# The recurrent block's weights split ahead of time and kept in DRAM, GpSimd taken out of that block, and the first gate's modulation summed on TensorE

## The chip, the core and the metric

One program on one core of a Trainium2 chip. The metric is the device time of one execution in microseconds (us). All matrix work is float32 in value: TensorE is fed pairs of `float32r` tiles (a high part and the remainder), three products for each pair of operands.

## The reference, cut to what matters

Two layers on a latent stream and a context stream of 256 tokens each, D = 1024. Layer 0 mixes by retention, layer 1 by a bidirectional gated linear recurrence (RG-LRU); each is followed by a gated ConvFFN. Every mixer and FFN is modulated by rows computed from `c`.

```python
for i in range(DEPTH):                       # DEPTH = 2; kind 0 = retention, kind 1 = RG-LRU
    mod_l = (silu(c) @ ada_w[i] + ada_b[i]); mod_c = silu(c_ctx) @ ada_w[i] + ada_b[i]
    sh1, sc1, g1, sh2, sc2, g2 = split(mod_l, 6)          # the same for the context
    h = rmsnorm(x, norm_mix[i]) * (1 + sc1) + sh1
    x = x + g1 * mixer(h)
    x = x + g2 * conv_ffn(rmsnorm(x, norm_ffn[i]) * (1 + sc2) + sh2)
return rmsnorm(x, final_norm)

def lru_mixer(h):                            # LRU_WIDTH = 1280, 8 blocks of 160
    y_br, x_br = split(h @ w_in, 2); x_br = dwconv4(x_br)
    for d in (forward, backward):
        r, i = sigmoid(block_diag(gate_w[d]) @ x_br + gate_b[d])
        log_a = -8 * r * softplus(-lam[d]); a = exp(log_a)
        h_d = scan(h_t = a_t * h_(t-1) + sqrt(-expm1(2 log_a)) * (i * x_br))
    return ((h_fwd + h_bwd) * gelu(y_br)) @ w_out
def conv_ffn(h): g, v = split(dwconv3(h @ w_up), 2); return (silu(g) * v) @ w_down
```

## The kernel before

All weights lie in DRAM as 128x128 blocks in the order in which TensorE uses them (`BLOCKS`, 1888 of them). Eight blocks make a **unit** (128x1024), two units a **piece** (1 MiB). SP loads pieces into four buffers `raw` (`load_pieces`). For each unit `unit_hi` copies `raw` to `whi`, rounding it, and `unit_lo` writes the remainder `wlo = raw - whi`; there are five buffers of each (`WBUFS`). `mm3` then issues the three matmuls (L431, L432, L433 in the trace). Outside of the recurrent block `prep_units` makes `whi` on ScalarE (ACT) and `wlo` on VectorE (DVE), two or three units ahead of TensorE (`ahead`).

The pieces of the modulation matrix `ada_w` (`ada`, 48 pieces) stand between the weight pieces. For all but the first eight of them (`k`), ACT multiplies each quarter of the piece by one column of silu(c) (`adap`, L486) and GpSimd (POOL) adds the products up (L487); a few matmuls against a one-hot column (L496) then sum over partitions. The groups are `g1`, `f0` in the retention, `l1`, `f1` in the first FFN (`ffn0`). Their work is handed out by `tick`, which every matmul group of eight blocks calls.

The recurrent block (`lru`) runs from 860 to 1038 us of the span. Its order on TensorE is written out by hand (`LRU_SEQ`: `x`, `y` projections, `g` gates, `s` a batch of square roots and gelus), then come 80 blocks of the output projection. Everything else there (convolution taps, gates, scans, and the splitting of the 40 units of weights) is placed by a small list scheduler (`Schedule`), which builds the order of each engine from costs in `add({"act": .., "dve": .., "pool": ..})` and due times; tasks that name several engines go to the one that it finds free. Each instruction stream is then executed in that order.

Of the kernel before, what the change touches and what calls it, by code (L numbers as in the profile page):

```python
# [12 lines left out]
P = 128  # L13
# [82 lines left out]
def make_plan():  # L96
# [57 lines left out]
    ffn(0)  # L154
    mat("lru_in", range(KD), [WCH + c for c in LRU_FIRST[:2]], True)
# [30 lines left out]
class Task:  # L186
    def __init__(self, alts, fn, deps=(), due=0.0, new=(), reads=()):
        self.alts, self.fn, self.deps, self.due = alts, fn, [d for d in deps if d], due
        self.new, self.reads, self.end = list(new), list(reads), None
        for b in self.reads:  # L190
            b.n += 1


class Schedule:
# [19 lines left out]
    def issue(self, t, e, at):  # L214
        self.free[e] = t.end = at + t.alts[e]
# [36 lines left out]
BLOCKS, PIECES = make_plan()  # L252
# [10 lines left out]
class Net:  # L263
    def __init__(self, ctx, tc, wpk, xt, cv, par, cst, out):
# [15 lines left out]
        self.ada_done, self.ada_sum = set(), {}  # L280

# [38 lines left out]
    def tick(self, n=1):  # L320
# [17 lines left out]
    def load_pieces(self, upto):  # L338
        while self.npiece <= min(upto, len(PIECES) - 1):
# [9 lines left out]
            n = PIECE if PIECES[i][0] == "ada" else min(PIECE, (len(BLOCKS) - PIECES[i][1]) * P)  # L349
# [42 lines left out]
    def unit_lo(self, e):  # L392
        r, hi = self.units[self.nlo]
# [6 lines left out]
        self.nlo += 1  # L400

# [12 lines left out]
    def blk(self, key, n=1):  # L414
# [9 lines left out]
        if key[0][:4] == "main":  # L424
            assert self.npiece <= self.piece_of[u // 2] + 4
# [31 lines left out]
    def pass_ada(self, pi):  # L457
        while self.npast < pi:
            p = PIECES[self.npast]
            if p[0] == "ada" and p[1] != "k":  # L460
                self.ada_piece(self.npast)
            self.npast += 1

    def ada_piece(self, pi):
# [12 lines left out]
        if half == 0:  # L477
# [11 lines left out]
        self.adaq.extend((pi, lambda s=s, j=j: product(s, j)) for j in range(4) for s in seqs)  # L489
# [8 lines left out]
        if half:  # L498
# [4 lines left out]
            if ns:  # L503
                self.adaq.append((pi, lambda: self.after(0 if name == "g1" else 5, lambda: total(ns))))
        if last:
# [15 lines left out]
            n = 1 if name == "g1" else 5  # L521
# [700 lines left out]
    def lru_body(self, pss, end):  # L1222
# [7 lines left out]
        steps, pos, est = [("l", [], self.pos - 16, 16, 5.2, 0.0)], self.pos, 5.2  # L1230
        for kind, *idx in LRU_SEQ:
            n, cost = {"x": (KD, 5.2), "y": (KD, 2.6), "g": (4, 0.0), "s": (0, 0.0)}[kind]
            if kind == "g":
                cost = 1.75 if idx[0] < LB else 3.2
            steps.append((kind, idx, pos, n, cost, est))
            pos, est = pos + n, est + cost
        for i, k in enumerate(LRU_OUT[:-2]):
            for m in range(KD - 1):
                steps.append(("o", (i, k, m), pos, 1, 0.33, est))
                pos, est = pos + 1, est + 0.33  # L1240
        for i, k in enumerate(LRU_OUT[:-2]):
            steps.append(("o", (i, k, KD - 1), pos, 1, 0.33, est))
            pos, est = pos + 1, est + 0.33
# [28 lines left out]
        def x_tasks(c, ps, dep):  # L1272
# [25 lines left out]
            a = add({"act": 0.57}, first, [dep], due - 4, [acc], [ps])  # L1298
            b = add({"dve": 2.0}, taps, [a], due - 3.5, [], [ps, acc])
            d = add({"act": 0.52, "dve": 0.45, "pool": 1.9}, fhi, [b], due - 1.4, [hi], [acc])  # L1300
            xt[c] = add({"dve": 0.6, "pool": 1.2}, flo, [d], due - 0.8, [lo], [acc, hi])
# [12 lines left out]
        def gate_tasks(c, d, prs, dep, at):  # L1314
# [378 lines left out]
```

## Time and profile before

| | |
|---|---|
| time, median of 3 runs (lowest, highest) | 1248.6 us (1247.59, 1250.68) |
| the profiled execution: its time, its span | 1248.26 us, 1246.5 us |
| TensorE (PE) busy | 1185.4 us (95%) |
| VectorE (DVE) busy | 913.2 us (73%) |
| ScalarE (ACT) busy | 724.9 us (58%) |
| GpSimd (POOL) busy | 509.8 us (41%) |
| DRAM read, written | 177.68 MB, 1.05 MB (143 GB/s over the span) |

The span is what the profile covers; 1.8 us of the execution's time lie around it. The shares are means over stages: TensorE is near 100% in most of the span and at 82% between 860 and 1038 us, so a stage has to be read by itself.

### The profile page before, as it was taken

The page shows a single profiled execution, that of the slowest core. Times are in us where ns is not written, and L with a number is a line of the kernel's source. Part 1 is how long each engine was busy: PE and PEld are TensorE (multiplying, and loading weights), DVE is VectorE, ACT ScalarE, POOL GpSimd, SP SyncE. Part 2 cuts the span into 40 slices and gives each one's busy share as a digit, 9 for nine tenths or more (in the row PEclk, how much of TensorE's full clock was granted, in tenths as well). Part 3 has the DMA queues.
Part 4 walks back from the last instruction along what each step waited for, and adds up shares of the span by engine and source line. Part 5 has one row for each costly group of instructions (what it writes and reads, how often), then busy time and mean ns, then how long its engine had stood idle before and what let it go on. Part 6 is the DMA issues. An engine that isn't in the chain of part 4 may idle for free.

```text
span 1246.5 us, 17524 instructions
## 1 busy us (share of the span) xinstructions
PE 1185.4 (95%) x6736; PEld 1010.0 (81%) x6736; DVE 913.2 (73%) x1271; ACT 724.9 (58%) x1101; POOL 509.8 (41%) x344
## 2 busy tenths in 40 slices
PE   8999999999989999999999999999995949999997
PEld 4787688788868898887788878799884848999996
DVE  5685974884693777998526776359999997988843
ACT  5496574756742445987536664245937816766642
POOL 0065673566330030999843652223656751000010
PEclk9999999999989999999999999999997979999998
DMA  9741452344242222556553553321423315455541
GB/s 330 298 170 62 135 174 100 132 169 169 68 132 71 71 99 71 200 180 214 214 195 142 203 191 116 132 68 53 176 71 119 141 68 169 170 188 184 202 137 35
DMA packets 33508, 181.44 MB, mean 146 GB/s; under 512 B 4240, under 2 KB 7952, under 8 KB 13328
## 3 DMA queue, kind: packets, MB, share of 16 engines
q1 hardware_dynamic: 32848, 179.79, 41.2%
q8 instruction: 53, 0.87, 0.3%
q10 hardware_dynamic: 576, 0.52, 0.1%
q14 instruction: 31, 0.25, 0.1%
HBM read 177.68 MB, written 1.05 MB: 143 GB/s over the span
## 4 chain that ended last, share of the span: by engine, by line
PE 70%; DVE 13%; issue 2%; ACT 2%; POOL 1%; DVEq 0%; ACTq 0%; POOLq 0%
PE ps L431 20%; PE ps L433 20%; PE ps L432 20%; PE ps L848 2%; PE ps L849 2%; PE ps L850 2%; DVE wlo L398 2%; DVE gp L1339 1%; DVE gp L1357 1%; DVE gp L1342 1%; DVE gp L1365 1%; DVE gp L1362 1%; PE av L432 1%; DVE whi L377 1%; PE av L431 1%
## 5 line engine op out<-in xcount | busy, mean ns | idle before, releaser
L487 POOL TENSOR_TENSOR ada<-ada,adap 128x512 f32<-128x512 f32 x224 | 361.0, 1639 | 284.6 <-ACT adap L486 253.3
L398 DVE TENSOR_TENSOR wlo<-raw,whi 128x1024 fp32r<-128x1024 f32 (+1 forms) x216 | 311.6, 1448 | 19.0 <-ACT whi L375 19.0
L375 ACT CAST whi<-raw 128x1024 fp32r<-128x1024 f32 (+3 forms) x219 | 219.9, 1016 | 60.8 <-PE ps L432 34.6
L433 PE MATMUL ps<-hhi,wlo 128*128 128x512 f32 (+1 forms) x640 | 243.7, 381 | 5.3 <-DVE wlo L398 5.3
L431 PE MATMUL ps<-hhi,whi 128*128 128x512 f32 (+1 forms) x640 | 247.5, 387 | 0.0
L432 PE MATMUL ps<-hlo,whi 128*128 128x512 f32 (+1 forms) x640 | 243.2, 380 | 0.0
L567 POOL TENSOR_TENSOR sq<-sq,sq 128x256 f32<-128x256 f32 x33 | 37.2, 1137 | 343.2 <-ACT sq L561 334.1
L432 PE MATMUL ps<-hx,whi 128*128 128x256 f32 x592 | 168.1, 284 | 0.4 <-DVE hx L600 0.2
L431 PE MATMUL ps<-hx,whi 128*128 128x256 f32 x592 | 168.2, 284 | 0.0
L433 PE MATMUL ps<-hx,wlo 128*128 128x256 f32 x592 | 167.5, 283 | 0.0
L431 PEld LDWEIGHTS ps<-hhi,whi 128*128 128x128 f32 x640 | 121.0, 189 | 30.8 <-issue 4.7
L486 ACT ACTIVATE adap<-raw,strip 128x512 f32<-128x512 f32 x224 | 144.2, 714 | 2.3 <-POOL ada L487 1.4
L433 PEld LDWEIGHTS ps<-hhi,wlo 128*128 128x128 f32 x640 | 120.9, 189 | 29.3 <-DVE wlo L398 6.2
L432 PEld LDWEIGHTS ps<-hlo,whi 128*128 128x128 f32 x640 | 121.0, 189 | 22.6 <-issue 1.0
L431 PEld LDWEIGHTS ps<-hx,whi 128*128 128x128 f32 x592 | 113.5, 192 | 4.0 <-issue 1.7
L432 PEld LDWEIGHTS ps<-hx,whi 128*128 128x128 f32 x592 | 113.5, 192 | 1.1 <-DVE hx L600 0.8
L433 PEld LDWEIGHTS ps<-hx,wlo 128*128 128x128 f32 x592 | 113.6, 192 | 0.0
L1090 DVE SCALAR_TENSOR_TENSOR cv<-ps,par,cv 128x510 f32<-128x510 f32 (+1 forms) x88 | 54.0, 613 | 64.0 <-ACT cv L1087 63.9
L1087 ACT ACTIVATE cv<-ps,par 128x512 f32<-128x512 f32 (+1 forms) x88 | 58.8, 669 | 71.4 <-PE ps L433 70.2
L398 POOL TENSOR_TENSOR wlo<-raw,whi 128x256 fp32r<-128x256 f32 (+3 forms) x30 | 58.6, 1958 | 44.7 <-PE ps L433 20.9
L431 PE MATMUL ps<-fzhi,whi 128*128 128x512 f32 (+1 forms) x198 | 72.9, 368 | 0.0
L432 PE MATMUL ps<-fzlo,whi 128*128 128x512 f32 (+1 forms) x198 | 72.4, 366 | 0.0
(208 smaller groups left out, 2372.5 us busy)
## 6 DMA issues: line engine op xcount, KB each, us to landing
raw<-wpk SPq DMA_DIRECT2D x157, 1024.0 KB, 5.0
ak<-wpk SPq DMA_DIRECT2D x32, 256.0 KB, 6.4
xc<-xt SPq DMA_DIRECT2D x4, 256.0 KB, 4.0
x<-xt SPq DMA_DIRECT2D x4, 256.0 KB, 5.7
raw<-wpk SPq DMA_DIRECT2D x2, 512.0 KB, 6.2
xst<-xhi SPq DMA_DIRECT2D x16, 64.0 KB, 2.0
cst<-cst SPq DMA_DIRECT2D x3, 192.0 KB, 5.0
cst<-cst SPq DMA_DIRECT2D x2, 256.0 KB, 5.3
```

The source lines that it names most:

```text
L375: self.nc.scalar.copy(dst, src)
L398: self.eng(e).tensor_tensor(d[q, o:n], r[q, o:n], hi[q, o:n].bitcast(F32), ALU.subtract)
L431: mm(ps, w[0], x[0], start=start, stop=False)
L432: mm(ps, w[0], x[1], start=False, stop=False)
L433: mm(ps, w[1], x[0], start=False, stop=stop)
L486: nc.scalar.mul(t, w, cs)
L487: nc.gpsimd.tensor_tensor(acc[i, s], acc[i, s], t, ALU.add)
L567: nc.gpsimd.tensor_tensor(self.acc[s], self.acc[s], sq, ALU.add)
L848: mm(pss[t], xh, wh, start=k == 0, stop=False)
L849: mm(pss[t], xh, wl, start=False, stop=False)
L1087: nc.scalar.activation(acc, ps[:, :n], AF.Identity, scale=w(1), bias=self.pc("fcb", layer * 44 + f))
L1090: nc.vector.scalar_tensor_tensor(a3[:, :, 1:], p3[:, :, :NS - 1], w(0), a3[:, :, 1:], ALU.mult, ALU.add)
```

## The change

Three things are changed.

1. The 20 pieces of the recurrent block (40 units) are no longer among the pieces that are split just before use. They are loaded as pieces `pre`, one for every 40 blocks from block 160 on, which is from early in the second head of the retention to late in `ffn0`. For each unit ACT makes the high part and DVE the remainder in a tile `pre` (two buffers), and SP writes both to a DRAM tile `kept` (1 MiB a unit). In the recurrent block `unit_hi` issues two DMAs, `whi` and `wlo` from `kept`, and nothing is left to do for `unit_lo`.
2. In the recurrent block no task names `pool` any more. The other costs of the scheduler are new numbers, and it gives another order.
3. For `g1` TensorE multiplies the `raw` tile by the columns of silu(c) and sums over partitions at once (16 matmuls); the products on ACT, the additions on POOL and the 4 one-hot matmuls of this group go.

```diff
+PRE = (160, 40)
@@ make_plan
+    early = {}
+    for n, i in enumerate(range(first, last, 16)):
+        early.setdefault((PRE[0] + PRE[1] * n) // 16 * 16, []).append(i)
...
+        pieces.extend(("pre", m) for m in early.get(i, []))
+        if not first <= i < last:
+            pieces.append(("blk", i))
@@ tick
+        if self.preq:
+            self.preq.popleft()[1]()
@@ unit_hi
+        if u in KEPT:
+            hi, lo = (self.wp.tile([P, UNIT], F32R, tag=f"w{n}", name=f"w{n}{u}") for n in ("hi", "lo"))
+            for j, t in enumerate((hi, lo)):
+                self.nc.sync.dma_start(t.bitcast(F32), self.kept[u][:, j, :])
...
+    def pre_piece(self, pi):
+        self.load_pieces(pi + 1)
+        r = self.raw[pi]
...
+        def hi(h, u):
+            st[h] = t = self.wp.tile([P, 2, UNIT], F32R, tag="pre", name=f"pre{u}", bufs=2)
...
+                    nc.scalar.copy(t[:, 0, o:a], r[:, h * UNIT + o:h * UNIT + a])
...
+        def lo(h, u):
+            t = st[h]
+            nc.vector.tensor_tensor(t[:, 1, :], r[:, h * UNIT:(h + 1) * UNIT], t[:, 0, :].bitcast(F32), ALU.subtract)
+            for kind, a, n in self.runs(u):
+                if kind == "left":
+                    nc.vector.tensor_copy(t[64:96, 0, a:n], t[64:96, 1, a:n])
...
+            nc.sync.dma_start(self.kept[u], st[h].bitcast(F32))
...
+        self.preq.extend((pi, f) for f in (
+            lambda: hi(0, u), lambda: (lo(0, u), hi(1, u + 1)), lambda: (lo(1, u + 1), keep(0, u)),
+            lambda: keep(1, u + 1)))
@@ ada_piece
+        if name == "g1":
+            for j in range(4):
+                nc.tensor.matmul(ps[32 * j:32 * j + 32, :], self.strip[:, half * 4 + j, 30 - 2 * i:62 - 2 * i],
+                                 r[:, j * 512:(j + 1) * 512], start=first, stop=last, tile_position=(0, 32 * j))
@@ scan_tasks, add_units
-            b = add({"dve": 0.6, "pool": 1.2}, fu, [dep, gt[c, d][1]], due - 4, [], [p, t])
+            b = add({"dve": 0.69}, fu, [dep, gt[c, d][1]], due - 4, [], [p, t])
...
-                    h = add({"act": 0.95, "dve": 0.85, "pool": 3.5}, lambda e: self.unit_hi(e), deps, due - 3)
...
+                    units[u] = add({"sp": 5.0}, lambda e: (self.unit_hi(e), self.unit_lo(e)), deps, due - 12)
```

How the orders move, at three places. First DVE in the third head of the retention, behind the reciprocal `rstd` of the head's norm; `wlo` are the weights that TensorE needs next, `zt` the head's output. Before:

```order
L581 RECIPROCAL rstd_2933<-sd_2931 128x512
L398 TENSOR_TENSOR wlo_2944<-raw_2675,whi_2882 128x1024
L398 TENSOR_TENSOR wlo_2983<-raw_2936,whi_2942 128x1024
L909 SCALAR_TENSOR_TENSOR zt_3021<-av_2818,par_87,rstd_2933 128x512
L910 TENSOR_TENSOR zt_3021<-zt_3021,sg_2535 128x512
```

Now:

```order
L648 RECIPROCAL rstd_2928<-sd_2926 128x512
L449 TENSOR_TENSOR pre_2903<-raw_2661,pre_2903 128x1024
L425 TENSOR_TENSOR wlo_2944<-raw_2771,whi_2873 128x1024
L425 TENSOR_TENSOR wlo_2983<-raw_2931,whi_2942 128x1024
L976 SCALAR_TENSOR_TENSOR zt_3021<-av_2809,par_89,rstd_2928 128x512
```

One remainder of a `pre` unit stands ahead of both `wlo`. Second, DVE in `ffn0`, in the stretch in which POOL adds up `l1` (`cv` are convolution taps, `fzlo` the split of the activations). Before:

```order
L1099 TENSOR_TENSOR cv_4824<-cv_4824,cv_4873 128x512
L398 TENSOR_TENSOR wlo_4881<-raw_4829,whi_4835 128x1024
L1090 SCALAR_TENSOR_TENSOR cv_4922<-ps_4878,par_87,cv_4922 128x2x255
L1091 SCALAR_TENSOR_TENSOR cv_4922<-ps_4878,par_87,cv_4922 128x2x255
L398 TENSOR_TENSOR wlo_4933<-raw_4829,whi_4879 128x1024
L454 TENSOR_TENSOR fzlo_4920<-cv_4824,fzhi_4919 128x512
```

Now:

```order
L1166 TENSOR_TENSOR cv_5116<-cv_5116,cv_5173 128x512
L425 TENSOR_TENSOR wlo_5181<-raw_5125,whi_5129 128x1024
L449 TENSOR_TENSOR pre_5170<-raw_5121,pre_5170 128x1024
L452 COPY pre_5170<-pre_5170 32x256
L1157 SCALAR_TENSOR_TENSOR cv_5226<-ps_5178,par_89,cv_5226 128x2x255
L1158 SCALAR_TENSOR_TENSOR cv_5226<-ps_5178,par_89,cv_5226 128x2x255
L449 TENSOR_TENSOR pre_5221<-raw_5121,pre_5221 128x1024
L452 COPY pre_5221<-pre_5221 32x256 x2
L425 TENSOR_TENSOR wlo_5244<-raw_5125,whi_5179 128x1024
L514 TENSOR_TENSOR fzlo_5224<-cv_5116,fzhi_5223 128x512
```

Two remainders stand between the two `wlo` of a weight piece. Third, the recurrent block: what SP issues behind the twelve small DMAs `xst`, which restack a projected chunk for the gates. Before:

```order
L1310 DMA xst_7515<-xhi_7472 32x512
L352 DMA raw_7532<-wpk 128x2048
L352 DMA raw_7622<-wpk 128x2048
L352 DMA raw_7723<-wpk 128x2048
L352 DMA raw_7787<-wpk 128x2048
```

Now:

```order
L1377 DMA xst_7694<-xhi_7641 32x512
L401 DMA whi_7756<-kept_2659 128x1024
L401 DMA wlo_7757<-kept_2659 128x1024
L401 DMA whi_7781<-kept_2936 128x1024
L401 DMA wlo_7782<-kept_2936 128x1024
L401 DMA whi_7817<-kept_2938 128x1024
```

SP now issues two DMAs of 512 KiB for each unit, where it issued one of 1 MiB for two units.

## Rows read from the trace of the kernel before

**Rows 1.** Waits of PE in the whole span: total us, times, longest us

```profile
PE ps L431 <- DVE lzz L377: 12.0, 1, 12.0
PE ps L431 <- DVE xhi L377: 11.9, 1, 11.9
PE ps L433 <- DVE wlo L398: 9.2, 6, 5.3
...
PE av L432 <- DVE plo L454: 3.1, 1, 3.1
...
PE ps L431 <- ACT xhi L375: 1.7, 1, 1.7
PE ps L432 <- DVE xlo L1296: 1.6, 2, 0.8
...
PE ps L431 <- DVE gy L377: 0.7, 1, 0.7
```

**Rows 2.** Stretches: us, busy of PE, PEld, DVE, ACT, POOL, PEclk, DMA, GB/s

```profile
225.00:262.00 37.00, 36.99 (x166) 29.34 (x165) 36.50 (x50) 24.73 (x40) 19.88 (x13) 1.00 0.38 124
328.00:356.00 28.00, 22.68 (x99) 18.34 (x98) 27.39 (x26) 20.49 (x33) 22.72 (x14) 0.94 0.44 147
...
499.00:592.00 93.00, 93.00 (x415) 76.07 (x414) 88.67 (x72) 77.66 (x117) 90.93 (x54) 1.00 0.58 198
...
860.00:1038.00 178.00, 145.18 (x986) 125.46 (x984) 173.20 (x206) 113.92 (x170) 106.68 (x72) 0.91 0.35 122
```

**Rows 3.** Timeline of PE in the recurrent block: start us, us, instruction

```profile
881.80 0.40 PE L431 MATMUL ps<-xhi,whi 128*128 128x512 f32 x1
...
883.66 0.40 PE L431 MATMUL ps<-xhi,whi 128*128 128x512 f32 x1
...
887.33 0.39 PE L431 MATMUL ps<-hx,whi 128*128 128x256 f32 x1
...
893.18 0.40 PE L431 MATMUL ps<-xhi,whi 128*128 128x512 f32 x1
```

**Rows 4.** Single lines on DVE, 857 to 1038 us: ns min/median/max, starts

```profile
L1287 DVE SCALAR_TENSOR_TENSOR xc<-ps,par,xc x19: 734/746/748, 857.0 to 950.3; 128x508 f32<-128x508 f32 x10, 128x510 f32<-128x510 f32 x9
L1339 DVE SCALAR_TENSOR_TENSOR gp<-gp,xc x20: 678/1016/2900, 872.9 to 996.1; 128x512 f32<-128x512 f32 x20
L1362 DVE TENSOR_TENSOR_SCAN gp<-ga,gp x10: 1209/1218/2030, 888.5 to 1024.1; 128x512 f32<-128x512 f32 x10
L1365 DVE TENSOR_TENSOR_SCAN gp<-ga,gp x10: 666/922/2305, 912.7 to 1025.2; 128x256 f32<-128x256 f32 x10
L1366 DVE TENSOR_TENSOR_SCAN gp<-ga,gp x10: 750/752/2648, 913.4 to 1026.4; 128x256 f32<-128x256 f32 x10
L1382 DVE TENSOR_TENSOR lz<-lz,gy x10: 392/412/952, 917.2 to 1028.9; 128x256 f32<-128x256 f32 x10
```

**Rows 5.** Groups by form on DVE, 499 to 561 us: busy us, mean ns, idle

```profile
L398 DVE TENSOR_TENSOR wlo<-raw,whi 128x1024 fp32r<-128x1024 f32 x11 | 24.6, 2234 | 0.0
```

**Rows 6.** The same on DVE, 1060 to 1122 us, where POOL stands still

```profile
L398 DVE TENSOR_TENSOR wlo<-raw,whi 128x1024 fp32r<-128x1024 f32 x22 | 26.8, 1217 | 0.0
```

**Rows 7.** POOL's additions for `g1`, 62 to 130 us: ns min/median/max, starts

```profile
L487 POOL TENSOR_TENSOR ada<-ada,adap x28: 1263/1392/2284, 68.7 to 126.7; 128x512 f32<-128x512 f32 x28
```

**Rows 8.** The chain that ended last, 315 to 357 us: start us, us

```profile
333.46 2.32 DVE wlo L398
...
353.19 2.30 DVE wlo L398
355.53 0.79 PE ps L433
```

**Rows 9.** The chain that ended last, 225 to 262 us: four one-hot matmuls

```profile
230.01 0.99 PE ada L496 x8
```

**Rows 10.** A stretch of loads at the start, columns as in rows 2

```profile
20.00:30.00 10.00, 9.98 (x56) 7.06 (x55) 5.60 (x18) 4.63 (x10) 0.00 (x0) 0.94 1.04 398
```

**Rows 11.** DMA issues: times, KB each, median us from issue to landing

```profile
raw<-wpk SPq DMA_DIRECT2D x157, 1024.0 KB, 5.0
```

More of the change, by code (lines that the diff above doesn't have):

```diff
@@ L154, in make_plan @@
     ffn(0)
+    first = len(blocks)
     mat("lru_in", range(KD), [WCH + c for c in LRU_FIRST[:2]], True)
@@ L168, in make_plan @@
     mat("lru_out", LRU_OUT[-2:], range(KD))
+    last = len(blocks)
     ffn(1)
-    assert len(blocks) % 8 == 0
+    assert len(blocks) % 8 == 0 and first % 16 == 0 and last % 16 == 0
+    early = {}
+    for n, i in enumerate(range(first, last, 16)):
+        early.setdefault((PRE[0] + PRE[1] * n) // 16 * 16, []).append(i)
     pieces = []
@@ L173, in make_plan @@
         pieces.extend(("ada",) + m for m in marks.get(i, []))
-        pieces.append(("blk", i))
-    assert sum(p[0] == "ada" for p in pieces) == 48
-    return blocks, pieces
+        pieces.extend(("pre", m) for m in early.get(i, []))
+        if not first <= i < last:
+            pieces.append(("blk", i))
+    assert sum(p[0] == "ada" for p in pieces) == 48 and sum(p[0] == "pre" for p in pieces) == (last - first) // 16
+    return blocks, pieces, range(first // 8, last // 8)
 class Buf:
@@ L188, in __init__ @@
         self.alts, self.fn, self.deps, self.due = alts, fn, [d for d in deps if d], due
-        self.new, self.reads, self.end = list(new), list(reads), None
+        self.new, self.reads, self.end, self.hold = list(new), list(reads), None, None
         for b in self.reads:
@@ L214, in issue @@
     def issue(self, t, e, at):
-        self.free[e] = t.end = at + t.alts[e]
+        t.end = at + t.alts[e]
+        self.free[e] = t.end if t.hold is None else at + t.hold
         for b in t.new:
@@ L249, in run @@
             self.issue(t, e, at)
[L252 removed]
+PRE = (160, 40)
+BLOCKS, PIECES, KEPT = make_plan()
 AH = (2, 3, 3)
@@ L280, in __init__ @@
         self.ada_done, self.ada_sum = set(), {}
+        self.preq = deque()
+        self.dp = ctx.enter_context(tc.tile_pool(name="dp", bufs=1, space=bass.MemoryType.DRAM))
+        self.kept = {}
     def slot(self, shape=None, dt=F32, name="t"):
@@ L348, in load_pieces @@
                 self.adaq.popleft()[1]()
-            n = PIECE if PIECES[i][0] == "ada" else min(PIECE, (len(BLOCKS) - PIECES[i][1]) * P)
+            while self.preq and self.preq[0][0] <= i - 4:
+                self.preq.popleft()[1]()
+            n = PIECE if PIECES[i][0] != "blk" else min(PIECE, (len(BLOCKS) - PIECES[i][1]) * P)
             r = self.wp.tile([P, PIECE], F32, tag="raw", name=f"raw{i}", bufs=4)
@@ L476, in ada_piece @@
         acc = self.ada_acc.setdefault(name, {})
-        if half == 0:
+        if half == 0 and name != "g1":
             acc.update({(i, s): self.slot(name="ada") for s in seqs})
@@ L497, in total @@
                                  start=n < 4, stop=n >= len(sums) - 4, tile_position=(0, 32 * j))
-        if half:
+        if half and name != "g1":
             done = [n for n, (b, s) in enumerate(sums) if b <= i]
@@ L503, in ada_piece @@
             if ns:
-                self.adaq.append((pi, lambda: self.after(0 if name == "g1" else 5, lambda: total(ns))))
+                self.adaq.append((pi, lambda: self.after(5, lambda: total(ns))))
         if last:
@@ L1228, in lru_body @@
         add = sch.add
-        steps, pos, est = [("l", [], self.pos - 16, 16, 5.2, 0.0)], self.pos, 5.2
+        steps, pos, est = [("l", [], self.pos - 16, 16, 5.8, 0.0)], self.pos, 5.8
         for kind, *idx in LRU_SEQ:
-            n, cost = {"x": (KD, 5.2), "y": (KD, 2.6), "g": (4, 0.0), "s": (0, 0.0)}[kind]
+            n, cost = {"x": (KD, 5.45), "y": (KD, 2.9), "g": (4, 0.0), "s": (0, 0.0)}[kind]
             if kind == "g":
-                cost = 1.75 if idx[0] < LB else 3.2
+                cost = 1.82 if idx[0] < LB else 3.4
             steps.append((kind, idx, pos, n, cost, est))
@@ L1296, in flo @@
                 self.eng(e).tensor_tensor(lo.t, acc.t, hi.t.bitcast(F32), ALU.subtract)
[L1298 to L1301, printed above, removed]
+            a = add({"act": 0.77}, first, [dep], due - 4, [acc], [ps])
+            b = add({"dve": 2.25}, taps, [a], due - 3.5, [], [ps, acc])
+            d = add({"act": 0.62, "dve": 0.42}, fhi, [b], due - 1.4, [hi], [acc])
+            xt[c] = add({"dve": 0.69}, flo, [d], due - 0.8, [lo], [acc, hi])
             if c >= LB:
```

79 lines of the change are left out of this document (48 added, 31 removed).

## The prediction

> **What bounds the kernel now.** I read the busy shares first, then the waits of TensorE, then stretches. TensorE is busy in 95% of the span, so the change can only win where TensorE stands still or runs below full clock, and can lose wherever it delays TensorE by a new wait. Its waits name the place: the two longest, 12.0 and 11.9 us, are for a high part of an activation made on DVE (`lzz`, `xhi`), and both lie in the recurrent block [rows 1]. The stretch of that block, 860 to 1038 us, shows why: DVE is busy for 173.2 of 178 us, PE for 145.2, and the granted clock is 0.91 on the mean against 1.00 in the others [rows 2]. So DVE is the bound there and nowhere else for long. Two other stretches matter because the change adds DVE work to them: 225 to 262 us (DVE 36.5 of 37) and 328 to 356 us (27.4 of 28) in the retention, and 499 to 592 us in `ffn0` (88.7 of 93, POOL 90.9), where TensorE does not wait at all [rows 2].
>
> **What the recurrent block could take at best.** The starts on TensorE give the issue intervals at full clock [rows 3]: 8 matmuls of a small gate take 883.66 - 881.80 = 1.86 us, the next gate, of the wide form, 887.33 - 883.66 = 3.67 us, and the 48 matmuls of 256 columns behind it 893.18 - 887.33 = 5.85 us, 0.122 each. By the code there are six x steps of 48 (35.1 us), ten y steps of 24 (29.3), 16 small gates (29.8), 4 wide ones (14.7) and 80 output blocks of 3 matmuls (29.3): 138 us. The stretch is 178 us, so 40 us are to be had: 33 of idling, and 7 in which the clock is down after the idling.
>
> **What DVE has left there.** All `whi` and `wlo` work goes; in exchange DVE gets back what POOL did (7 products of the drive, 4 `xlo`, some `lz`). How long these take when POOL is silent is not a guess: in the same stretch the shortest one of each kind shows it, 0.75 us a tap, 0.68 for a 128x512 operation where the median is 1.02 and the longest 2.90, 1.21 for a forward scan, 0.92 and 0.75 (I take the medians) for the halves of a backward one, 0.41 for a 128x256 operation [rows 4]. With the counts of the new order: 30 taps 22.4, 10 `xlo` and 60 operations on `gp` 70 x 0.68 = 47.6, 10 forward scans 12.1, 10 backward 16.7, 30 on `lz` and `lzz` 12.3, 11 small casts and copies 3.5: 115 us. That is less than TensorE's 138, so TensorE becomes the bound. The tail holds too: behind the last gate's first DVE operation the new order has some 25 us of DVE work, and TensorE still has 32 us (one y step and the output blocks).
> Not all waits vanish. Those for ACT's `xhi`, for `xlo` and for `gy`, 1.7 + 1.6 + 0.7 = 4.0 us [rows 1], are latencies of a chunk through two engines and I keep them: the block then takes 142 us, and the term is **-36 us**. Bounds: -40 with no wait at all; -24 if only the two long waits go.
>
> **What the early split costs.** Forty units need one cast on ACT and one subtraction on DVE each, between 155 and 745 us. A subtraction takes 2.23 us while POOL adds up [rows 5] and 1.22 us when it stands still [rows 6].
> In `ffn0`, 499 to 592 us, three pieces fall (at blocks 592, 640, 672): six subtractions, 6 x 2.23 = 13.4 us, into 93 - 88.7 = 4.3 us of DVE idling [rows 2, 5]. The rest, 9.1 us, makes the `wlo` late, and by the order shown above they stand directly ahead of one. Weights are prepared two to three units ahead, and some of that lead can pay, but DVE is full for the whole stretch, so the lead is spent once. I take **+9 us**; from below 6 x 1.22 - 4.3 = 3.0, from above 13.4 and no idling used.
> This is where a rule of the Trainium skill speaks against the change: SBUF — State Buffer, Who interferes with whom, says that a DVE instruction with two SBUF inputs contends with a GpSimd instruction that reads SBUF, and that the loser waits for the whole instruction of the other. By it a subtraction would cost 1.22 plus at most one addition, 1.39 us in the median [rows 7], 2.6 us, and the term would be 6 x 2.6 - 4.3 = 11.3 us; the row's 2.23 us agrees with the rule's direction and I go by the row.
> In the retention, two subtractions stand ahead of the weights used at about 248 us, in a stretch with 0.5 us of DVE idling [rows 2], and one ahead of the `wlo` at 333 us, which is on the chain that ended last and leads without a gap to the 2.3 us `wlo` that PE starts behind at 355.5 us [rows 8]. Three uncovered subtractions at 1.22 to 2.3 us are 3.7 to 6.9 us; two more at 258 us may add up to 4.6. I take **+6 us**; bounds 3.7 and 11.5. The other pieces fall where DVE has room; should that cover be gone, each subtraction costs 1.2 to 2.2 us.
> The casts on ACT (about 1 us each) I cost at nothing: in its fullest stretch ACT is busy 77.7 of 93 us [rows 2] and six more casts fit. The 16 short copies beside the remainders are hidden with them or belong to the bounds.
>
> **The first gate.** Four f32 matmuls of this kind take 0.99 us [rows 9]. Sixteen in place of four cost 3 us of TensorE, which has no room: +3. Against it: the 28 additions on POOL, 1.39 us each in the median, end, the last one at 127 us [rows 7]; the wait of 3.1 us for `plo` [rows 1] lies in their midst, among DVE operations that POOL stretches, and should go. I take **0**; bounds -4 (more of the stretching is on the path) and +3 (the wait stays).
>
> **The transfers.** SP moves 40 MiB into DRAM early and 40 MiB back in the block; 36 units, 38 MB, within 142 us are 266 GB/s. At the start the queues carry 398 GB/s, with rows of 8 KB and shorter [rows 10], so a unit needs about 2.7 us and TensorE uses one in 3.9 us on the mean, with five in flight. In `ffn0` the DMA engines are busy 0.58 at 198 GB/s [rows 2]; 3 MiB more in each 27 us (116 GB/s) bring that to 0.92. I cost transfers at nothing there; what it would cost if loads come late is in the rivals. SP's queue is in order: a write `kept` that waits for its remainder holds the next weight load. The raw buffers are loaded about two units ahead, so a few us of that are covered.
>
> **The sum** is made against the profiled execution, 1248.3 us (0.3 under the median): 1248.3 - 36 + 9 + 6 + 0 = **1227 us**.
>
> **Rivals.**
> *The early work is hidden.* If the lead of the weights pays for both early stretches, only 0 to 3 us remain of the 15: 1248.3 - 36 + 2 = 1214 us. For it: PE has no wait at all in 499 to 592 us. Against it: DVE is full there and POOL's work does not shrink. Chance 0.14.
> *The block finds a new wait.* Once DVE is free, ACT (113.9 of 178 us busy [rows 2], and nearly the same work in 142), the `xst` DMAs behind eighteen unit loads on SP's queue, or the tail may hold TensorE; then only the 24 us of the two long waits come back: 1248.3 - 24 + 15 = 1239 us. Chance 0.18.
> *Slower: the loads feed the block.* A unit needs a free pair of buffers; if the queue gets no more than one unit moving at a time, each costs the 5.0 us that 1 MiB takes from issue to landing [rows 11], 36 x 5.0 = 180 us, plus some 2 us for the first: the block takes 182 where it took 178, and the early 15 us are paid as well: 1248.3 + 4 + 15 = 1267 us. It decides from (178 - 15) / 36 = 4.5 us a unit. Against it stand five buffers and 398 GB/s. Chance 0.05.
> *It does what it says and gives it all back.* Early losses at their upper bounds (13.4 + 11.5 + 3) and the block's gain at its lower: 1248.3 - 24 + 28 = 1252, and near it the cases within 0.3%. Chance 0.04.
> *The forecast*, 1220 to 1235 us by its own terms: 0.59.
>
> **Numbers.** About 0.3%, 3.7 us, is what a measurement of this kernel can tell from no change. The range 1212 to 1242 holds the forecast, the hidden case and most of the new-wait case. Faster 0.90 (the forecast, the first two rivals, less a little of the second), same 0.04, slower 0.06.
>
> **What would show it.** Right: between about 875 and 1017 us of the new span (its start moved by the early 15 us) DVE is busy around 115 of 142 us, its 128x512 operations at 0.68 us, PE waits there under 8 us, and the clock is 1.00. In 499 to 592 us PE waits for `wlo`, 9 us in sum, and again at 248 and 355 us. At 103 us the wait for `plo` is gone. Wrong: PE waiting for DMA `whi` or `wlo` in the block (the loads are too slow); no wait for `wlo` in `ffn0` (hidden); waits for ACT or `xst` in the block; or ACT waiting for `raw` behind a `kept` write, a cost that I set to nothing.

## The result, and the profile after

The changed kernel takes 1257.16 us (median of 6 runs, 1255.81 to 1258.7), the kernel before 1250.05 us on the same chip (6 runs, 1247.59 to 1253.56): a ratio of 1.0057, interval 1.0039 to 1.0074. It is slower by 0.57%, where 1227 us were forecast, 1212 to 1242 as the range, and slower with a chance of 0.06.

First the page of the changed kernel: busy time, memory traffic, the chain that ended last by engine, and three groups.

```profile
PE 1196.5 (95%) x6760; PEld 1014.0 (81%) x6760; DVE 887.3 (71%) x1285; ACT 728.9 (58%) x1098; POOL 352.6 (28%) x242
...
HBM read 219.62 MB, written 42.99 MB: 209 GB/s over the span
...
PE 64%; DVE 14%; ACT 9%; DMA 8%; issue 3%; SPq 1%; POOL 0%; DVEq 0%; ACTq 0%
...
L549 POOL TENSOR_TENSOR ada<-ada,adap 128x512 f32<-128x512 f32 x196 | 312.7, 1619 | 384.9 <-ACT adap L548 356.0
L425 DVE TENSOR_TENSOR wlo<-raw,whi 128x1024 fp32r<-128x1024 f32 x196 | 276.7, 1416 | 31.5 <-ACT whi L392 31.3
L392 ACT CAST whi<-raw 128x1024 fp32r<-128x1024 f32 x196 | 203.4, 1043 | 160.0 <-DMA raw<-wpk 136.5
```

DVE and GpSimd do less, as intended, but ACT now stands for 136.5 us before its casts, waiting for a weight load (16.7 us in the kernel before). Next the waits of TensorE in the whole span (total us, times, longest), which answer to [rows 1]:

```profile
PE ps L493 <- DVE wlo L425: 37.8, 17, 5.2
PE st L638 <- POOL sq L634: 3.5, 3, 1.7
PE ps L491 <- ACT fzhi L513: 2.2, 1, 2.2
...
PE ps L491 <- ACT lzz L392: 1.3, 1, 1.3
```

The two waits of 12 us for high parts made on DVE are gone, and so is the one for `plo`; that for `wlo` has grown from 9.2 to 37.8 us; 3.6 us of it lie between 140 and 165 us, behind the first gate. Stretches of the changed kernel, columns as in [rows 2]; the first is the recurrent block:

```profile
908.00:1048.00 140.00, 138.20 (x979) 122.14 (x979) 104.62 (x172) 106.49 (x159) 2.29 (x2) 0.99 0.79 279
499.00:531.00 32.00, 32.00 (x142) 26.48 (x142) 23.51 (x25) 22.28 (x33) 13.93 (x10) 1.00 0.52 198
531.00:561.00 30.00, 24.07 (x85) 18.76 (x84) 28.93 (x24) 21.98 (x34) 23.86 (x14) 0.83 0.65 245
561.00:594.00 33.00, 29.06 (x123) 22.34 (x122) 28.41 (x23) 21.95 (x33) 29.93 (x19) 0.95 0.66 245
594.00:630.00 36.00, 29.80 (x124) 23.75 (x123) 28.27 (x24) 25.29 (x37) 26.88 (x18) 0.95 0.65 239
```

The block did what was forecast: 140 us in place of 178, DVE 104.6 us, clock 0.99. In `ffn0`, where TensorE was busy throughout before [rows 2], it now stands still for 5.9 us of 30, 3.9 of 33 and 6.2 of 36, and the granted clock of these stretches is 0.83, 0.95 and 0.95 on the mean, part of the time at the lower of its two levels (1.2 GHz in place of 2.4).

**Where the time went, matmul by matmul.** Order and number of the 5922 matmuls that `mm3` issues (three in each of 1974 calls) are the same in all kernels here. So I took the start of the k-th in each trace and subtracted its start in the kernel before. The table gives that lateness in us, with k and the start before. A trace is one execution, which lies up to 2.7 us from the median of its kernel (4.6 us in `d_raw5` below), so a lateness can differ by that much from what the medians say.

| k | before | changed | place |
|---|---|---|---|
| 424 | 160.2 | -1.3 | behind the first gate |
| 627 | 225.1 | -0.1 | retention |
| 1060 | 345.1 | +11.0 | behind the retention's full stretches |
| 1716 | 491.0 | +10.6 | before the stretch of `l1` in `ffn0` |
| 2165 | 594.0 | +35.9 | in it |
| 2917 | 769.1 | +47.9 | later `ffn0` |
| 3817 | 918.2 | +48.0 | recurrent block, its first part |
| 4788 | 1100.1 | +10.4 | `ffn1` |

So the block gains 48.0 - 10.4 = 37.6 us, and the early work has cost 48.0 us by then, 11 in the retention and 37 in `ffn0`; 15 were forecast. How a loss arises is seen in the chain of the changed kernel, 525 to 565 us (start us, us, what):

```profile
540.90 2.21 DVE pre L449
543.12 2.22 DVE wlo L425
545.34 0.02 issue
545.36 7.70 DMA raw<-wpk
553.06 0.02 issue
553.08 1.05 ACT whi L392
```

and in SP's queue, 520 to 620 us (start, us from first to last, instruction, number):

```profile
523.33 10.04 SPq L369 DMA_DIRECT2D raw<-wpk  x2
539.37 4.14 SPq L456 DMA_DIRECT2D kept<-pre  x2
543.60 31.82 SPq L369 DMA_DIRECT2D raw<-wpk  x7
578.45 5.14 SPq L456 DMA_DIRECT2D kept<-pre  x2
583.64 21.37 SPq L369 DMA_DIRECT2D raw<-wpk  x5
```

A remainder of an early piece stands ahead of a running block's `wlo` on DVE; the raw buffer that this `wlo` frees is what the next load waits for; and the load is one of three that go out together behind two writes. It takes 7.7 us from issue to landing. All loads of 499 to 594 us, beside the writes (times, KB, median us to landing):

```profile
raw<-wpk SPq DMA_DIRECT2D x15, 1024.0 KB, 7.0
kept<-pre SPq DMA_DIRECT2D x6, 1024.0 KB, 4.4
```

and the loads of the same stretch in the kernel before:

```profile
raw<-wpk SPq DMA_DIRECT2D x17, 1024.0 KB, 5.0
```

What this does to ACT shows in the groups of its casts, 499 to 769 us, before and after:

```profile
L375 ACT CAST whi<-raw 128x1024 fp32r<-128x1024 f32 x49 | 50.9, 1043 | 26.6 <-PE ps L432 15.7 <-DMA raw<-wpk 10.9
```

```profile
L392 ACT CAST whi<-raw 128x1024 fp32r<-128x1024 f32 x43 | 44.9, 1045 | 69.9 <-DMA raw<-wpk 69.8
```

I also matched each load with the first cast that reads it. In the kernel before, the median weight piece had landed 28 us ahead of that cast between 345 and 491 us, but only 1.8 us ahead between 491 and 594 us and 2.4 us between 594 and 769; in the changed kernel the last two are 0.0.

What of it decides can't be told from one trace: the writes, the ring of four raw buffers, the transfers themselves, or DVE's work. The theories in the runs below: **1** the writes hold SP's queue, **2** a piece occupies one of the four raw buffers, **3** the DMA engines have no room, **4** DVE's remainders, stretched by GpSimd's additions, come late.

### The profile page after: what moved, and what is told of

It is laid out like the page before. It is cut to its first block, busy times and chain, and to the rows that moved or that the text cites. A ratio compares the mean times of both kernels' runs of the same rounds, so it can differ in the third digit from the quotient of the medians.

```text
span 1256.9 us, 17610 instructions
## 1 busy us (share of the span) xinstructions
PE 1196.5 (95%) x6760; PEld 1014.0 (81%) x6760; DVE 887.3 (71%) x1285; ACT 728.9 (58%) x1098; POOL 352.6 (28%) x242
## 4 chain that ended last, share of the span: by engine, by line
PE 64%; DVE 14%; ACT 9%; DMA 8%; issue 3%; SPq 1%; POOL 0%; DVEq 0%; ACTq 0%
PE ps L491 17%; PE ps L493 17%; PE ps L492 17%; DMA raw<-wpk 7%; DVE wlo L425 3%; ACT adap L548 3%; PE ps L915 2%; PE ps L916 2%; PE ps L917 2%; DVE pre L449 2%; ACT whi L392 1%; PE av L492 1%; PE av L491 1%; PE av L493 1%; DVE rstd L648 1%
## 5 line engine op out<-in xcount | busy, mean ns | idle before, releaser
L549 POOL TENSOR_TENSOR ada<-ada,adap 128x512 f32<-128x512 f32 x196 | 312.7, 1619 | 384.9 <-ACT adap L548 356.0
L425 DVE TENSOR_TENSOR wlo<-raw,whi 128x1024 fp32r<-128x1024 f32 x196 | 276.7, 1416 | 31.5 <-ACT whi L392 31.3
L392 ACT CAST whi<-raw 128x1024 fp32r<-128x1024 f32 x196 | 203.4, 1043 | 160.0 <-DMA raw<-wpk 136.5
L493 PE MATMUL ps<-hhi,wlo 128*128 128x512 f32 (+1 forms) x640 | 248.3, 388 | 26.3 <-DVE wlo L425 26.3
L491 PE MATMUL ps<-hhi,whi 128*128 128x512 f32 (+1 forms) x640 | 251.0, 392 | 0.0
L492 PE MATMUL ps<-hlo,whi 128*128 128x512 f32 (+1 forms) x640 | 246.7, 385 | 0.3 <-DVE hlo L667 0.3
L548 ACT ACTIVATE adap<-raw,strip 128x512 f32<-128x512 f32 x196 | 126.0, 713 | 0.0
L493 PE MATMUL ps<-fzhi,wlo 128*128 128x512 f32 (+1 forms) x198 | 73.1, 369 | 0.0
```

The lines of the kernel that those rows point to most:

```text
L392: self.nc.scalar.copy(dst, src)
L425: self.eng(e).tensor_tensor(d[q, o:n], r[q, o:n], hi[q, o:n].bitcast(F32), ALU.subtract)
L491: mm(ps, w[0], x[0], start=start, stop=False)
L492: mm(ps, w[0], x[1], start=False, stop=False)
L493: mm(ps, w[1], x[0], start=False, stop=stop)
L548: nc.scalar.mul(t, w, cs)
```

## The experiments

"Lateness" is that of matmul 3817, just in the recurrent block, as in the table (changed kernel 48.0). Ratios are against the kernel before on the same chip.

**No early work** (`a_noearly`): only the first piece stays.

```
-    for n, i in enumerate(range(first, last, 16)):
+    for n, i in enumerate(range(first, first + 16, 16)):
...
-                self.nc.sync.dma_start(t.bitcast(F32), self.kept[u][:, j, :])
+                self.nc.sync.dma_start(t.bitcast(F32), self.kept[KEPT[0] + u % 2][:, j, :])
```

> Leaves out 19 of the 20 early pieces (load, cast, remainder, write); the recurrent block reads the two units of the one piece that is kept again and again, so its weights are wrong and its transfers as many as before. All theories: the loss of the early work, 11 us in the retention and 38 us in ffn0 by the two traces, goes, and the block's gain of 38 us stays: 1257 - 48 = 1209 us, within 4. If the block is faster only because it begins late and finds its units already loaded, its gain shrinks and the time is 1220 us or more.

1208.65 us, ratio 0.967 (0.9651 to 0.9689), lateness -0.2, as expected. The whole loss belongs to the early work, and the block's gain does not hang on it.

**No writes** (`b_nowrite`), with the same reading of one piece and:

```
-            nc.sync.dma_start(self.kept[u], st[h].bitcast(F32))
+            if u // 2 == KEPT[0] // 2:
+                nc.sync.dma_start(self.kept[u], st[h].bitcast(F32))
```

> Loads and splits all 20 pieces as the changed kernel does, but writes only the first one to DRAM; the recurrent block reads that one again and again (wrong weights, as many transfers). Theory 1 (the writes hold SP's queue: a write waits for its remainder and the next loads stand behind it) and theory 3 (the 40 MiB of writes take the DMA engines' time): most of the ffn0 loss goes, 1257 - 25 to 33 = 1224 to 1232 us. Theory 2 (each piece occupies one of the four raw buffers for some 20 us) and theory 4 (the remainders on DVE beside POOL): at most 5 us go, 1252 us or more.

1241.04 us, 0.9929 (0.9909 to 0.995), lateness 30.5: between the two. The writes cost 17.5 us; 30.5 stay. Loads now land in 4.9 us in 499 to 594 us.

**Writes later** (`c_late`); `both` writes the two halves, at the latest at the next piece's first step.

```
+        def late():
+            self.lastkeep = both
+            self.after(2, both)
...
-            lambda: hi(0, u), lambda: (lo(0, u), hi(1, u + 1)), lambda: (lo(1, u + 1), keep(0, u)),
-            lambda: keep(1, u + 1)))
+            lambda: hi(0, u), lambda: (lo(0, u), hi(1, u + 1)), lambda: lo(1, u + 1), late))
```

> Both writes of a piece are issued together two ticks after the second remainder, when they wait for nothing; nothing is left out. Theory 1 (the waiting write holds the loads): most of the ffn0 loss goes, 1225 to 1235 us. Theories 2 (raw buffers), 3 (DMA time) and 4 (DVE work): no more than 5 us go, 1252 us or more.

1289.46 us, 1.032 (1.0297 to 1.0342). No theory expected that, and the run does not decide: the edit brought a wait of its own. ACT's waits, 180 to 860 us (total, times, longest):

```profile
ACT whi L393 <- DMA raw<-wpk: 129.0, 26, 11.6
ACT pre L444 <- DMA kept<-pre: 22.5, 4, 9.0
```

The two `pre` buffers are still being written when the next piece's cast wants them, and ACT, which also makes every running `whi`, waits.

**Five raw buffers** (`d_raw5`):

```
-        self.nslot = 56
+        self.nslot = 52
...
-            r = self.wp.tile([P, PIECE], F32, tag="raw", name=f"raw{i}", bufs=4)
+            r = self.wp.tile([P, PIECE], F32, tag="raw", name=f"raw{i}", bufs=5)
```

> Five raw buffers in place of four (and 52 slots in place of 56); nothing is left out. Theory 2 (a piece occupies one of four buffers, so the weight loads behind it come late): most of the ffn0 loss goes, 1222 to 1235 us. Theory 1 (SP held by a waiting write): the loads still stand behind the write in the queue, but the one ahead of it is out one piece sooner, so some 5 to 12 us go, 1245 to 1252 us. Theories 3 and 4: no change, 1253 to 1261 us.

1254.32 us, 1.0036 (1.0023 to 1.0048): some 3 us under the changed kernel, with intervals that overlap. The lateness, 47.7, is that of the slowest of its ten executions, 1258.9 us. SP's waits, 490 to 770 us, of this run:

```profile
SPq L369 <- DVE wlo L425: 83.9, 15, 9.5
SPq L456 <- DVE pre L452: 69.5, 7, 22.2
SPq L456 <- DVE pre L449: 67.1, 11, 12.0
```

and of the changed kernel, at the writes:

```profile
SPq L456 <- DVE pre L449: 48.6, 11, 7.2
SPq L456 <- DVE pre L452: 39.6, 7, 14.0
```

With a buffer more, the queue stands before the writes (L456) instead: 136.6 us in place of 88.2.

**No writes and five buffers** (`e_nowrite_raw5`), the two edits together.

> As the run without writes (1241 us; it leaves out 19 of 20 pieces' writes), with five raw buffers in place of four. That run still lost 21 us in ffn0 and 9 in the retention. Theory 2 (the four-buffer ring brings the weights late): ffn0's 21 us fall to 5 or less, 1222 to 1227 us; then five buffers alone gave only 3 us because the waiting writes held the queue. Theory 4 (remainders and casts on DVE and ACT): 1237 us or more.

1238.38 us, 0.9911 (0.9896 to 0.9926), lateness 29.2, where theory 4 had it. Theory 2 alone fails.

**No writes and small remainders** (`f_nowrite_tiny`); the short copies are cut in the same way:

```
-            nc.vector.tensor_tensor(t[:, 1, :], r[:, h * UNIT:(h + 1) * UNIT], t[:, 0, :].bitcast(F32), ALU.subtract)
+            n = UNIT if u // 2 == KEPT[0] // 2 else 32
+            nc.vector.tensor_tensor(t[:, 1, :n], r[:, h * UNIT:h * UNIT + n], t[:, 0, :n].bitcast(F32), ALU.subtract)
```

> As the run without writes, with the early remainders of 19 pieces computed for 32 of 1024 columns only (and the small copies for 32): every wait and hand-over stays, DVE's work of the split goes (the parts left out are not stored anywhere). Theory 4 (DVE's work): nearly all of the 30 us go, 1211 to 1219 us. Theory 2 (ring of four): ffn0's 21 us stay for the most part, 1230 us or more, and only the retention's 9 may go.

1228.31 us, 0.9833 (0.9808 to 0.9858), lateness 18.0: between both. The retention's loss goes almost whole (at matmul 1060 from 9.2 to 1.9), in `ffn0` 16 us stay.

**Own buffer and queue** (`g_side`): the pieces leave `load_pieces`. Not printed here: a tick takes two steps of a piece where more than five wait, and the buffer is paid for with four slots, as in `d_raw5`.

```
+    def load_pre(self):
...
+            r = self.wp.tile([P, PIECE], F32, tag="side", name=f"side{i}", bufs=1)
+            self.nc.scalar.dma_start(r, self.d_w[i])
...
-            nc.sync.dma_start(self.kept[u], st[h].bitcast(F32))
+            nc.scalar.dma_start(self.kept[u], st[h].bitcast(F32))
...
-            lambda: hi(0, u), lambda: (lo(0, u), hi(1, u + 1)), lambda: (lo(1, u + 1), keep(0, u)),
-            lambda: keep(1, u + 1)))
+            lambda: hi(0, u), lambda: (lo(0, u), hi(1, u + 1)), lambda: lo(1, u + 1),
+            lambda: (keep(0, u), self.load_pre()), lambda: keep(1, u + 1)))
```

> Nothing left out: the early pieces get a buffer of their own (52 slots in place of 56), their loads and writes are issued from ACT's queue, the writes a tick or two after the remainder; SP's queue and the four raw buffers serve the running blocks alone, as before the change. DVE and ACT do the same work, the DMA engines move the same bytes. Theories 1 and 2 (queue and ring): ffn0's 38 us fall to about the 9 of the prediction, 1225 to 1232 us. Theory 3 (40 MiB more moved beside the loads) 1245 us or more; theory 4 (DVE's work) 1245 us or more.

1242.43 us, 0.9948 (0.9929 to 0.9967), lateness 33.2; faster than both kernels, but only half of what theories 1 and 2 expected. ACT's wait for running loads is nearly gone (first row, 180 to 860 us; 121.7 us in the changed kernel), and TensorE still waits for `wlo` (second, 499 to 630 us):

```profile
ACT whi L392 <- DMA raw<-wpk: 7.9, 6, 2.4
...
PE ps L502 <- DVE wlo L427: 14.5, 6, 4.8
```

Stretches of this run, columns as above:

```profile
499.00:530.00 31.00, 31.00 (x139) 25.66 (x138) 25.68 (x24) 24.32 (x35) 19.38 (x11) 1.00 0.65 236
530.00:560.00 30.00, 23.68 (x90) 18.63 (x89) 27.57 (x23) 21.19 (x32) 23.67 (x15) 0.89 0.67 241
560.00:592.00 32.00, 29.57 (x125) 22.74 (x124) 30.96 (x26) 24.43 (x36) 29.93 (x18) 0.95 0.87 331
592.00:630.00 38.00, 32.29 (x130) 25.82 (x129) 36.34 (x30) 26.36 (x40) 29.69 (x19) 0.91 0.68 252
```

and DVE's groups for the pieces, 499 to 592 us:

```profile
L458 DVE TENSOR_TENSOR pre<-side,pre 128x1024 fp32r<-128x1024 f32 x8 | 16.2, 2026 | 0.0
...
L461 DVE CAST pre<-pre 32x256 fp32r<-32x256 f32 x4 | 5.1, 1266 | 0.1
```

DVE is the fullest engine beside TensorE here: 27.57 us of 30, 30.96 of 32 and 36.34 of 38. That its work is the limit is shown by `l_side_nopool` and `m_side_l1` below.

**Small remainders, no writes, five buffers** (`i_nowrite_tiny_raw5`), all three edits.

> Both cuts at once: no writes and remainders of 32 columns for 19 of 20 pieces (left out, as in the runs before), and five raw buffers. Without writes, five buffers alone gave 3 us and small remainders alone 13 of the 30 us. Theory 5 (two limits side by side: the ring of four brings the weights late, and DVE's added work makes their remainders late; taking one away leaves the other): together nearly all goes, 1210 to 1215 us. Theory 3 (the DMA engines cannot carry 20 MiB more of loads there): five buffers add nothing, 1225 us or more.

1221.28 us, 0.9764 (0.9749 to 0.9778), lateness 10.1, between the two; the direction is that of two limits side by side, and 10 us stay unnamed.

**A quiet GpSimd, own queue** (`l_side_nopool`), and the same cut in the changed kernel (`n_nopool`) and in the kernel before (`o_before_nopool`, but for `g1`):

```
-                nc.gpsimd.tensor_tensor(acc[i, s], acc[i, s], t, ALU.add)
+                nc.gpsimd.tensor_tensor(acc[i, s][:, :32], acc[i, s][:, :32], t[:, :32], ALU.add)
```

> The run with its own buffer and queue (1242 us), with GpSimd's additions for the modulation cut to 32 of 512 columns (the rest of the sums is left out). Theory 4 (with the queue freed, what is left is DVE's work, stretched by GpSimd): a remainder takes 1.2 in place of 2.2 us, the 25 us left in ffn0 fall to 5 or less and the retention's 8 to 4 or less, 1213 to 1222 us. Theory 3 (DMA time) 1236 us or more.

1198.58 us, 0.959 (0.957 to 0.9609), lateness -12.9: below what was expected, since 11 of it belong to the kernel before (below). DVE's groups, 475 to 580 us:

```profile
L427 DVE TENSOR_TENSOR wlo<-raw,whi 128x1024 fp32r<-128x1024 f32 x18 | 22.4, 1243 | 0.0
...
L458 DVE TENSOR_TENSOR pre<-side,pre 128x1024 fp32r<-128x1024 f32 x10 | 12.6, 1257 | 0.0
...
L461 DVE CAST pre<-pre 32x256 fp32r<-32x256 f32 x7 | 2.0, 292 | 0.2
```

> The changed kernel with GpSimd's additions cut to 32 of 512 columns (the rest of the sums is left out); ring, queue and writes as in the changed kernel. If DVE under GpSimd's additions is the root and the ring and the waiting writes only hand its lateness on: as with the own queue, 1199 to 1206 us. If ring and queue cost by themselves, the 15 us that the own queue gave stay: 1211 to 1219 us.

1227.79 us, 0.9826 (0.9809 to 0.9843), lateness 17.9. Ring and queue do cost by themselves, 29 us between this run and the last, twice what was expected; ACT's wait, 180 to 860 us, is about that of the changed kernel (121.7):

```profile
ACT whi L392 <- DMA raw<-wpk: 118.0, 26, 10.5
```

> The kernel before with the same cut of GpSimd's additions for the later three vectors (left out; the first gate's stay whole). The own-queue run without them was 13 us ahead of the kernel before already in the retention. If that gain belongs to the cut and not to the change, this kernel has it too, 1233 to 1239 us, and the change is worth its whole 38 us when GpSimd is quiet; if the gain needs the change, 1247 us or more.

1239.21 us, 0.9917 (0.9902 to 0.9932), lateness -11.4. The gain belongs to the cut.

**Other places for the pieces**, with the own queue (`j_side_moved`) and without (`k_moved`):

```
-PRE = (160, 40)
+PRE = (144, 176, 368, 392, 416, 440, 464, 488, 512, 688, 720, 752, 784, 816, 848, 880, 912, 944, 960, 976)
...
-        early.setdefault((PRE[0] + PRE[1] * n) // 16 * 16, []).append(i)
+        early.setdefault(PRE[n] // 16 * 16, []).append(i)
```

> Nothing left out: the run with its own buffer and queue, and the 20 pieces placed where that run lost nothing: two at blocks 144 and 176, seven from 368 to 512, eleven from 688 to 976, none in 192 to 352 and in 528 to 672. Theory 4 (DVE's full stretches are what costs): the 33 us of early loss fall to 10 or less, 1209 to 1220 us. Theory 3 (a piece costs transfers wherever it stands): denser pieces make it no better, 1235 us or more.

1238.32 us, 0.9897 (0.9882 to 0.9912), lateness 26.1: not what theory 4 wanted, and in the range given for theory 3.

> Nothing left out: the changed kernel with only the places of the 20 pieces changed in the same way; ring of four and SP's queue as they are. If the place decides (DVE and the running loads have room there), the 48 us fall to some 15, 1220 to 1230 us. If the ring and the waiting writes cost by themselves wherever a piece stands, 1240 us or more.

1264.54 us, 1.0108 (1.0093 to 1.0123), lateness 54.3, as said for a ring and writes that cost wherever a piece stands. Denser pieces cost where none had cost before: with the own queue 14 us between 345 and 491 us of the kernel before, without it 17 there and 33 from 594 to 918. In the first of these stretches ACT stood longer for DMAs than with the pieces in their old places: with the own queue 18.3 us for the pieces' loads and 5.8 for their writes (6.5 and 3.6 in `g_side`), without it 24.7 us for running loads (8.4 in the changed kernel). So this does not speak for theory 3, since with the own queue the DMA engines were busy for 0.40 to 0.69 of it, but points at the single buffer and the ring; no run separates them. These places are no way out; `r_side_l1_moved` below tries others.

**The vector `l1` on TensorE** (`m_side_l1`), on top of the own queue, and all three vectors (`p_side_all`):

```
+        direct = name in ('g1', 'l1')
...
-        if name == "g1":
+        def four():
             for j in range(4):
...
+        if name == "g1":
+            four()
+        elif direct:
+            self.adaq.append((pi, four))
```

> Nothing left out: own buffer and queue for the early pieces, and the 12 pieces of the vector l1 (those of the stretch 490 to 640 us) summed on TensorE directly like the first gate's, 4 f32 matmuls of together 0.99 us a piece, so neither ACT's products nor GpSimd's additions stand there. If GpSimd's additions there are the cause of the 25 us that the own-queue run (1242 us) still loses in ffn0: 1242 - 25 + 12 = 1229 us, within 5. If not: 1242 + 12 = 1254 us.

1228.81 us, 0.9835 (0.9819 to 0.985), lateness 20.5. Three stretches of this run:

```profile
499.00:530.00 31.00, 31.00 (x144) 23.80 (x143) 24.05 (x31) 16.74 (x22) 0.00 (x0) 1.00 0.69 242
530.00:560.00 30.00, 30.00 (x142) 22.05 (x141) 18.43 (x23) 11.46 (x16) 0.00 (x0) 1.00 0.84 327
560.00:592.00 32.00, 32.00 (x148) 24.62 (x147) 22.53 (x28) 18.35 (x23) 0.00 (x0) 1.00 0.83 312
```

TensorE is busy throughout at full clock while the DMA engines move 312 to 327 GB/s, more than the 198 to 245 of the changed kernel there. That rules theory 3 out for this stretch, and so does `l_side_nopool`, with the transfers of `g_side` and TensorE busy for 130.8 of 131 us between 499 and 630 us. What `ffn0` still loses, 20.5 - 9.5 = 11 us, is about the added matmuls, 12 x 0.99 [rows 9].

> Nothing left out: as the run before, with all three later vectors summed on TensorE, 36 pieces. If GpSimd's additions cost what the run without them showed (1199 us), this is 1199 + 36 x 0.99 = 1234 us, within 6; if TensorE hides some of these matmuls in waits that it has anyway, 1220 to 1228 us; if the additions were not the cause, 1270 us or more.

1229.61 us, 0.9842 (0.9826 to 0.9859): the two are alike, and within the 6 us of the first forecast. At matmul 1716 it is 14.5 us ahead of `m_side_l1`, the matmuls of `f0` paid; those of `f1` and what stands beside them take 13.5 of it between matmuls 2165 and 2917.

**Writes or ring?** `n_nopool` with the edit of `b_nowrite` (`s_quiet_nowrite`), and with that of `d_raw5` (`t_quiet_raw5`).

> The changed kernel with a quiet GpSimd (1228 us; additions of 32 of 512 columns) and without 19 of 20 pieces' writes (both left out; the block reads one piece again and again). If the writes in SP's queue, ahead of the running loads, are what still costs 29 us there, 1199 to 1209 us. If the ring of four buffers costs by itself, 1218 us or more.

1214.77 us, 0.9717 (0.9694 to 0.9739), lateness 1.2: between the two.

> The changed kernel with a quiet GpSimd (same part left out), with its writes, and five raw buffers in place of four. If the ring of four costs by itself, 1199 to 1209 us. If the writes ahead of the loads in the queue do, 1222 us or more. Half each: 1212 to 1218 us.

1218.5 us, 0.9754 (0.9732 to 0.9775), lateness 7.0, about half each. Both share in it: by the lateness the writes with 16.7 us and a fifth buffer with 10.9, by the medians with 13 and 9.

**No pieces in the retention** (`r_side_l1_moved`), on top of `m_side_l1`:

```
-PRE = (160, 40)
+PRE = (368, 32)
```

> Nothing left out: the run with own queue and buffer and the vector l1 on TensorE (1229 us), with the pieces from block 368 on, one in 32 blocks, so none in the retention's full stretches. If the retention's 8 us go and the denser pieces find room, 1218 to 1223 us. If the denser transfers cost as much as the retention did, 1227 us or more.

1225.59 us, 0.9804 (0.9781 to 0.9826), lateness 13.3, between the two: the retention's loss is gone (-0.2 at matmul 1060). Its interval overlaps that of `m_side_l1`, so whether it is better stays open. Either is faster than the kernel before by 1.6 to 2%.

## Why the prediction was wrong

By its own steps, in us:

| step | forecast | measured | how |
|---|---|---|---|
| recurrent block | -36 | -37.6 | 48.0 to 10.4 in the table |
| first gate | 0 | -1.3 | matmul 424; held in the rows below |
| retention, three remainders | +6 | +8.3 | `g_side`, matmul 1060; 11.0 with the transfers of the changed kernel |
| `ffn0`, six remainders | +9 | +24.9 | `g_side`, 8.3 at matmul 1060 to 33.2 |
| transfers | 0 | +14.8 | 48.0 - 33.2 |

The second row left out, the measured ones add up to 10.4, the lateness at matmul 4788.

**Right.** The block's term and its reasons: 140 us against the 142 forecast, DVE 104.6 us against 115, TensorE's waits there 2.9 us. DVE's rows, 908 to 1048 us, are those short ones that [rows 4] promised:

```profile
L1406 DVE SCALAR_TENSOR_TENSOR gp<-gp,xc 128x512 f32<-128x512 f32 x20 | 13.7, 688 | 11.6 <-ACT gp L1396 11.6
L1429 DVE TENSOR_TENSOR_SCAN gp<-ga,gp 128x512 f32<-128x512 f32 x10 | 12.2, 1218 | 0.1
```

The first gate and, within its bounds, the retention were right too; of the retention's loss 7.3 us are the remainders (`f_nowrite_tiny`). One row was misread: the clock is not 1.00 in all stretches outside the block, it is 0.94 in 328 to 356 us, where TensorE is busy for 22.7 of 28 us [rows 2]. None of the rivals came true as told; "gives it all back" has nearly the time, 1252 us, but through upper bounds of terms that were not what failed most, and with the block's gain at its lower end.

**Wrong, first: transfers at nothing.** The step that failed is "the raw buffers are loaded about two units ahead, so a few us of that are covered". They were not: between 491 and 769 us the median load of the kernel before landed some 2 us before its first cast, and three casts already waited for theirs, 10.9 us in sum. A piece takes one buffer of four until its second remainder, and its two writes stand ahead of the next loads. Bandwidth, which I had looked at, was not the limit in `ffn0` (`m_side_l1`, `l_side_nopool`); order and the ring were (`g_side` moves the same bytes). The changed kernel loses 12.0 us of this between matmuls 2165 and 2917, behind the stretch that the prediction priced; without the writes it is 0.8. The sentence under "Wrong" named the sign, ACT waiting for `raw`, and gave it no price.

**Wrong, second: the size of `ffn0`'s +9.** I counted six remainders by the blocks at which the pieces stand. In the own-queue run eight fall into 499 to 592 us, 16.2 us, and the copies that I called hidden take 5.1 more, 1.27 us each beside GpSimd. Between matmuls 1716 and 2165 of that run there are nine remainders, 19.6 us, and seven copies, 8.9 us. TensorE stood there for 14.5 us, waiting for `wlo`, and ran slower behind the waits, which the term left out: the clock was 0.89, 0.95 and 0.91 on the mean of 30, 32 and 38 us, 3.3 + 1.6 + 3.4 = 8 us. Together that is about the 23.5 us lost between these two matmuls. The sign "9 us in sum" in 499 to 592 us came out by luck: TensorE idled for 9.9 us there, but in the new span that window ends 38 us before the stretch does. By the rule of the Trainium skill (SBUF — State Buffer, Who interferes with whom) that the prediction weighed, a remainder would take up to 2.6 us; the trace agrees in direction, with 2.03 us on the mean and 2.32 at most beside GpSimd's additions and 1.26 on the mean where they are cut.

**The two limits lie side by side**, which is why each removal alone looked small. Lateness at matmul 3817:

| | GpSimd adds | GpSimd cut |
|---|---|---|
| kernel before | 0 | -11.4 |
| changed kernel | 48.0 | 17.9 |
| changed, own queue and buffer | 33.2 | -12.9 |

With both gone nothing is lost against the kernel before with the same cut (-12.9 against -11.4). Queue and ring cost 14.8 us while GpSimd adds and 30.8 when it is quiet; beyond the 11.4 us that they cost the kernel before, the additions cost the changed kernel 48.0 - (17.9 + 11.4) = 18.7 us with the shared queue and 33.2 + 1.5 = 34.7 with its own. That each limit hides part of the other is read from this table: freeing the queue gives 14.8 us, cutting the additions 48.0 - 17.9 = 30.1, both together 48.0 + 12.9 = 60.9. A sum of terms, each priced with the others at rest, can't show this.

Not settled: what the 10 us of `i_nowrite_tiny_raw5` are, and why writes cost 17 us in the shared queue, split into the transfer ahead of a load and SP's waiting; `c_late` was to show the latter and didn't.

## What to carry to other kernels

Before a new consumer joins a ring of buffers, read from the trace how long a load has landed before its first use; where that is little (2 us here), a buffer held longer or a transfer put ahead in the queue can be lost time, whatever share of bandwidth is free. Give rare side work its own buffer and queue. Where one removal gives little, remove two suspects at once before calling either innocent.

## What the runs showed of the hardware

GpSimd's additions cost the kernel before 11 us of lateness, 3.5 of them by matmul 424, though its one wait for `wlo` in the retention's stretches (225 to 360 us) is 5.3 us: cutting them to 32 columns is worth a ratio of 0.9917 by itself. A copy of 32x256 on DVE takes 1.27 us on the mean beside them and 0.29 when they are cut; the taps `cv`, which read PSUM, take 0.75 us either way. TensorE pays twice for a wait: in 531 to 561 us of the changed kernel it idled for 5.9 us and the granted clock was 0.83 on the mean, against 1.00 in the 32 us ahead, where it did not idle. Loads of 1 MiB land 7.0 us after their issue where writes of the same size stand ahead, 5.0 before and 4.9 without the writes; but in `m_side_l1` and `l_side_nopool` they take 8.3 and 8.2 us in 499 to 594 us while TensorE is busy throughout (93.0 and 92.8 of 93 us), so the time to landing alone is not the loss.
